# The last two token pairs before a block-product stage: two operand rests formed by TensorE and ScalarE

## The chip, the cores and the metric

The kernel runs on one core of one Trainium2 chip. The metric is the device time of one execution in microseconds, median over several runs. The engines are TensorE (PE, matmuls into PSUM), VectorE (DVE), ScalarE (ACT), GpSimd (POOL) and SyncE (SP, which issues most DMAs). Each engine works through its own instructions in a fixed order, and semaphores tie the engines together.

## The reference

Two layers of a sequence model over 1024 tokens of width 1024, in float32. Each layer has a token mixer (an S5 state-space mixer with a gated linear unit in layer 0, a gated short convolution in layer 1), a SwiGLU feed-forward block of hidden width 2816, and an embedding gated by the residual stream. Every part takes an RMS-normed copy of the residual stream `h` and adds its result to it:

```python
def swiglu_ffn(u, w_in, w_out):
    gate, up = jnp.split(u @ w_in, 2, axis=-1)
    return (jax.nn.silu(gate) * up) @ w_out
...
    for i in range(DEPTH):
        ...
        h = h + mix
        h = h + swiglu_ffn(rmsnorm(h, norm_ffn_g[i]), ffn_w_in[i], ffn_w_out[i])
        gate = jax.nn.sigmoid(rmsnorm(h, norm_ple_g[i]) @ ple_w_gate[i])
        h = h + gate * (p[i] @ ple_w_up[i])
```

## The kernel before

**Products in three terms.** A float32 operand x is kept as a pair: `hi`, x rounded to the type `fp32r` that PE multiplies, and the rest `lo = x - hi`. A product is then three matmuls (`mm3`, lines 124 to 126): hi by hi, hi by lo, lo by hi. `split` (line 89) makes such a pair: ACT casts x to `hi` (line 90), then DVE subtracts to give `lo` (line 91). Elsewhere, in the state-space part and for the embeddings, `split_pe` (line 289) makes it without DVE from an x that lies in PSUM: ACT casts (291), PE adds minus the identity times `hi` onto the same PSUM bank (292), ACT copies what is left to SBUF (293).

**Block products.** Three stages multiply by a large weight through a Strassen-like scheme of seven block products in place of eight: the input product of both feed-forward blocks (`ffn_in`) and that of the short convolution (`conv_in`). The moving side is the normed, transposed residual stream. The 1024 tokens are eight tiles of 128; tile q and tile q + 4 form pair q, and the 1024 channels are split in two halves. So each pair has four blocks p[row, half], each 128x512 in one PSUM bank, and from these come seven operands: p00; T2; T1; p01; T3; p11; T4, with b12 a copy of p10, T1 = b12 - p00, T2 = p11 - T1, T3 = p11 - b12, T4 = p01 - T2. Counted from 0, operand 3 is p01 (the fourth) and operand 5 is p11 (the sixth). `put(c, q, src)` (line 227) splits operand c of pair q into its place: operands 0 to 3 in `ulow`, 4 to 6 in `uhigh`. One product of `block_product` (line 349) reads one operand of all four pairs at once (512 columns), 12 matmuls for four slices of channels. Seven products accumulate in three PSUM banks a, b, c; the fourth product accumulates onto bank a after ACT has copied the first product out of it (lines 364 and 375).

The stationary side comes from `weights_set` (line 315): two raw tiles give seven weight operands in the same way, with four DVE additions (lines 335, 336, 338, 343) and seven splits (lines 90 and 91, tile name `ws`).

**Handing over from the stage before.** The stage ahead of each block-product stage finishes `h` tile by tile. `posted` (line 1314) then norms each tile and, once both tiles of a pair are there, `norm_pair` (line 220) makes that pair's operands beside the matmuls of the other tiles. Pairs 0 and 1 go this way. Pairs 2 and 3 (a and z) are left for `last_pairs` (line 256), which runs when the stage's last matmuls are over. It transposes (`transposed`, line 182, on PE with an identity, into PSUM), puts operand 0 of each pair, and steps two generators `others` (line 230) in turn: one step per operand from 1 to 6. It runs three times: ahead of the first feed-forward block, of the convolution and of the second feed-forward block.

PSUM tiles come from the pools `tr` (three banks) and `mm` (five banks, line 1290); the products' a, b, c come from `mm` too, and p01 of pair a and p00 and p01 of pair z lie there. The tiles b12, T1, T2, T3 and T4 share one SBUF pool `t2` with five buffers (line 1306).

**What sets the order.** The order of the instructions on each engine is not that of the code. A planner in the launch (line 1423, `schedule_with_timeline_sim=True`) works it out by a simulated timeline: earlier code has priority, `first()` and `tc.high_priority` raise it, and an instruction is placed once what it needs is there on that timeline. `tc.issue_after(ins)` forces the instructions in its block behind `ins` on that engine. `last_pairs` notes its last ACT instruction (`done["others"]`, line 271), and `weights_set` places the first weight operand of the stage's second set behind it (line 331). The first set's raw tiles are loaded ahead of the stage and its first operands have a raised priority.

Of the kernel before, what the change touches and what calls it, by code (L numbers as in the profile page):

```python
# [14 lines left out]
ALU = mybir.AluOpType  # L15
# [3 lines left out]
P = 128  # L19
# [5 lines left out]
def trunk(  # L25
# [8 lines left out]
    V, A, G, PE = nc.vector, nc.scalar, nc.gpsimd, nc.tensor  # L34
# [21 lines left out]
    ident = const.tile([P, P], F32, name="ident")  # L56
# [10 lines left out]
    KH = KT // 2  # L67
# [17 lines left out]
    def psum(pool=None):  # L85
        pool = pool or mm
        return pool.tile([P, 512], F32, name="ps" + pool.name, tag="ps")

    def split(hi, lo, src):
        A.copy(hi, src)  # L90
        V.tensor_tensor(lo, src, hi.bitcast(F32), ALU.subtract)  # L91
# [62 lines left out]
    def t2_tile(name, dt=F32, n=512):  # L154
        return t2.tile([P, n], dt, name=name, tag="t2")
# [14 lines left out]
    def normed(t, gb, halves=1, xn=None):  # L170
        with first():
            rs = norm_stat(t)
            if xn is None and early:
                turn.append(turn.pop(0))
                xn = raw_tile(turn[-1], name="xn")
            xn = raw_tile(name="xn") if xn is None else xn
            for c in range(halves):
                cs = slice(c * D // halves, (c + 1) * D // halves)
                V.scalar_tensor_tensor(xn[:, cs], h[t][:, cs], rs, gb[:, cs], ALU.mult, ALU.mult)
        return xn  # L180

    def transposed(xn, hf, pool=None):

        pt = psum(pool or tr)
        for c in range(KH):
            kt = hf * KH + c
            PE.transpose(pt[:, c * P:(c + 1) * P], xn[:, kt * P:(kt + 1) * P], ident)
        return pt

    def by_kt(a):  # L190
        return a.rearrange("p (c j) -> p c j", c=KH)
# [17 lines left out]
    def moving_part(c, l, q):  # L209

        if c < 4:
            return ulow[:, q].rearrange("p (c k l j) -> p c k l j", c=4, k=KH, l=2)[:, c, :, l, :]
        return uhigh[:, c - 4, :, l, q * P:(q + 1) * P]
# [6 lines left out]
    def norm_pair(q, gb):  # L220
        x0, x1 = normed(q, gb), normed(q + HT, gb)
        p = {(0, 0): transposed(x0, 0), (1, 0): transposed(x1, 0), (1, 1): transposed(x1, 1), (0, 1): transposed(x0, 1, mm)}
        put(0, q, p[0, 0])
        for _ in others(q, p):
            pass

    def put(c, q, src):
        split(moving_part(c, 0, q), moving_part(c, 1, q), by_kt(src))

    def others(q, p):  # L230

        b12 = t2_tile("b12")
        A.copy(b12, p[1, 0])
        T1 = t2_tile("T1")
        V.tensor_tensor(T1, b12, p[0, 0], ALU.subtract)
        T2 = t2_tile("T2")
        V.tensor_tensor(T2, p[1, 1], T1, ALU.subtract)
        put(1, q, T2)
        yield
        put(2, q, T1)  # L240
        yield
        put(3, q, p[0, 1])
        yield
        T3 = t2_tile("T3")
        V.tensor_tensor(T3, p[1, 1], b12, ALU.subtract)
        put(4, q, T3)
        yield
        put(5, q, p[1, 1])
        yield
        T4 = t2_tile("T4")  # L250
        V.tensor_tensor(T4, p[0, 1], T2, ALU.subtract)
        put(6, q, T4)

    done = {}

    def last_pairs(xs, gb):


        a, z = HT - 2, HT - 1
        with tc.issue_after(done["sum"]), tc.issue_after(done["square"]):  # L260
            p = {(0, 0): transposed(xs[a], 0), (1, 0): transposed(xs[a + HT], 0), (1, 1): transposed(xs[a + HT], 1),
                 (0, 1): transposed(xs[a], 1, mm)}
            put(0, a, p[0, 0])
            xs[z], xs[T - 1] = normed(z, gb, 2), normed(T - 1, gb, 2)
            r = {(0, i): transposed(xs[z], i, mm) for i in range(2)}
            put(0, z, r[0, 0])
            r.update({(1, i): transposed(xs[T - 1], i) for i in range(2)})
            pa, pz = others(a, p), others(z, r)
            for g in (pa, pa, pz, pz, pa, pz, pa, pz, pa, pz, pa, pz):
                next(g, None)  # L270
            done["others"] = next(i for i in reversed(tc.nc.cur_bb.bb.instructions) if i.engine == A.engine)
# [12 lines left out]
    def transposes(pt, parts):  # L284
        for c, a in enumerate(parts):
            PE.matmul(pt[:, c * P:(c + 1) * P], a, ident, start=c == 0, stop=True, is_transpose=True,
                      skip_group_check=c > 0)

    def split_pe(hi, lo, pt, view=lambda a: a):

        A.copy(hi, view(pt))
        PE.matmul(pt, identn, hi, start=False, stop=True, skip_group_check=True)
        A.copy(lo, view(pt))
# [568 lines left out]
    def small(shape=(P, NG), dt=F32):  # L862
        return st.tile(list(shape), dt, name="sm", tag="sm", bufs=28)
# [8 lines left out]
    def tt(o, a, b, op):  # L872
        V.tensor_tensor(o, a, b, op)
        return o
# [68 lines left out]
    for hf in range(2):  # L943
        pt = psum(tr)
# [5 lines left out]
    for hf in range(2):  # L950
        pt = psum(tr)
# [22 lines left out]
    r = small()  # L974
# [7 lines left out]
    z = tt(small(), r, r, ALU.mult)  # L982
# [331 lines left out]
    def posted(gain, pairs):  # L1314

        gb = load_gain(gain)
        xs = {}

        def post(t):
            if not pairs:  # L1320
                return norm_tile(t, gb)
            spill(t)
            if 0 < t < HT - 1:
                norm_pair(t - 1, gb)
            elif t == HT - 1:
                xs.update({i: normed(i, gb) for i in (HT - 2, T - 2)})
            elif t == T - 1:
                last_pairs(xs, gb)
        return post
# [98 lines left out]
```

## Time and profile before

| | us |
|---|---|
| median of 3 runs | 2269.39 |
| lowest and highest run | 2267.07, 2272.16 |
| the profiled execution | 2269.76 |
| its span, first to last instruction | 2267.8 |
| busy in the span: PE, DVE, ACT, POOL | 2168.0, 1644.6, 908.5, 358.7 |

Times in the profile's rows count from the start of the span. A row of the timeline gives the start, the duration, the engine, the line, the operation, output <- input, and in brackets the engine's idle time just before, with what ended it. A row of a group gives the count, the busy time with the mean duration of one, and the idle time before them. Buffer numbers are left out of names: `psmm` and `pstr` are tiles of the PSUM pools `mm` and `tr`, `T` stands for T1 to T4, `ws` for weight operands, `st` for sums of weights, `raw` for loaded weights. PE matmuls overlap, so their spacing, not their duration, is what one costs on a busy PE; the same holds to a smaller extent for DVE and ACT.

### The profile page before, as it was taken

The numbers are of one execution on the slowest core, as the hardware profiler recorded it, in microseconds if no ns is written. First come the engines' busy times: TensorE is split into PE (matmuls) and PEld (weight loads), VectorE is DVE, ScalarE is ACT, GpSimd is POOL, SyncE is SP. The second block draws the span as 40 slices with busy tenths as digits, with TensorE's granted clock in tenths as the row PEclk, the third lists the DMA queues.
The fourth block names the chain that finished last, engine by engine and source line by source line (L and its number), as shares of the span: only waits on it lengthen the run. The fifth ranks groups of instructions, "written<-read, shape, count | busy, mean of one in ns | idle before, by whom it ended". The sixth has DMA issues, their size and how long they took to land. (4 is left out here: it accounts for less than half of the span.)

```text
span 2267.8 us, 27890 instructions
## 1 busy us (share of the span) xinstructions
PE 2168.0 (96%) x10001; PEld 1785.5 (79%) x10001; DVE 1644.6 (73%) x2746; ACT 908.5 (40%) x1731; POOL 358.7 (16%) x440
## 2 busy tenths in 40 slices
PE   6997999899999999999979999989999999999998
PEld 5776888788888877878858888868888888787887
DVE  7785324877777787887588776497877777778864
ACT  6554322444444443335343332263444444333442
POOL 2111001011111112342010000110111111224210
PEclk8999999999999999999989999999999999999999
DMA  7655301344444477664232333723444445866713
GB/s 242 159 121 136 110 19 47 110 163 146 164 143 158 148 247 295 242 243 160 98 107 84 93 93 123 263 97 121 154 152 150 157 146 190 327 255 224 256 60 112
DMA packets 234010, 358.14 MB, mean 158 GB/s; under 512 B 23696, under 2 KB 166032, under 8 KB 233872
## 3 DMA queue, kind: packets, MB, share of 16 engines
q1 hardware_dynamic: 203040, 247.24, 33.6%
q0 software_dynamic: 30432, 109.08, 13.6%
q8 instruction: 79, 1.29, 0.2%
q14 instruction: 59, 0.48, 0.1%
q10 hardware_dynamic: 400, 0.04, 0.0%
HBM read 225.53 MB, written 114.29 MB: 150 GB/s over the span
## 5 line engine op out<-in xcount | busy, mean ns | idle before, releaser
L124 PE MATMUL psmm<-ulow,ws 128*128 128x512 f32 x896 | 352.3, 394 | 19.0 <-ACT ws L90 17.6
L126 PE MATMUL psmm<-ulow,ws 128*128 128x512 f32 x896 | 351.0, 392 | 3.1 <-DVE ws L91 3.1
L125 PE MATMUL psmm<-ulow,ws 128*128 128x512 f32 x896 | 351.7, 393 | 0.0
L124 PE MATMUL psmm<-uhigh,ws 128*128 128x512 f32 x672 | 261.4, 389 | 0.0
L125 PE MATMUL psmm<-uhigh,ws 128*128 128x512 f32 x672 | 261.4, 389 | 0.0
L126 PE MATMUL psmm<-uhigh,ws 128*128 128x512 f32 x672 | 261.4, 389 | 0.0
L90 ACT CAST ws<-raw 128x512 fp32r<-128x512 f32 x224 | 138.7, 622 | 265.8 <-PE psmm L126 245.6
L487 POOL DMA_DIRECT2D hw<-hs x154 | 115.9, 753 | 767.8 <-DVE hs L91 741.6
L124 PEld LDWEIGHTS psmm<-ulow,ws 128*128 128x128 f32 x896 | 170.3, 190 | 56.5 <-ACT ws L90 18.8
L126 PEld LDWEIGHTS psmm<-ulow,ws 128*128 128x128 f32 x896 | 169.8, 189 | 40.8 <-DVE ws L91 5.4
L125 PEld LDWEIGHTS psmm<-ulow,ws 128*128 128x128 f32 x896 | 170.2, 190 | 35.1
L629 DVE TENSOR_TENSOR h<-psmm,h 128x512 f32<-128x512 f32 x234 | 155.2, 682 | 45.6 <-PE psmm L126 25.6
L638 POOL TENSOR_TENSOR h<-part,h 128x512 f32<-128x512 f32 x100 | 139.1, 1394 | 242.6 <-ACT part L637 213.1
L124 PE MATMUL psmm<-ulow,w 128*128 128x512 f32 x380 | 150.8, 397 | 14.6 <-DVE h L629 10.0
L91 DVE TENSOR_TENSOR ws<-raw,ws 128x512 fp32r<-128x512 f32 x224 | 153.4, 687 | 4.7 <-ACT ws L90 4.6
L126 PE MATMUL psmm<-ulow,w 128*128 128x512 f32 x380 | 148.1, 390 | 0.0
L125 PE MATMUL psmm<-ulow,w 128*128 128x512 f32 x380 | 148.0, 389 | 0.0
L124 PEld LDWEIGHTS psmm<-uhigh,ws 128*128 128x128 f32 x672 | 126.2, 188 | 26.2
L125 PEld LDWEIGHTS psmm<-uhigh,ws 128*128 128x128 f32 x672 | 126.2, 188 | 26.1
L126 PEld LDWEIGHTS psmm<-uhigh,ws 128*128 128x128 f32 x672 | 126.2, 188 | 26.1
L90 ACT CAST ws<-st 128x512 fp32r<-128x512 f32 x168 | 103.8, 618 | 102.2 <-PE psmm L126 94.9
L124 PE MATMUL psmm<-w,ulow 128*128 128x512 f32 (+1 forms) x360 | 139.0, 386 | 0.0
(266 smaller groups left out, 4435.9 us busy)
## 6 DMA issues: line engine op xcount, KB each, us to landing
hw<-hs POOLq DMA_DIRECT2D x154, 512.0 KB, 4.2
w<-hw SPq DMA_DIRECT2D x88, 768.0 KB, 5.6
raw<-in_ffn_w_in_dram SPq DMA_DIRECT2D x88, 512.0 KB, 3.9
raw<-in_ffn_w_out_dram SPq DMA_DIRECT2D x44, 512.0 KB, 6.3
hd<-h POOLq DMA_DIRECT2D x24, 512.0 KB, 3.0
h<-hd SPq DMA_DIRECT2D x24, 512.0 KB, 5.9
raw<-in_conv_w_in_dram SPq DMA_DIRECT2D x24, 512.0 KB, 4.0
w<-hw SPq DMA_DIRECT2D x88, 128.0 KB, 5.5
```

The costliest lines, as they stand in the source:

```text
L90: A.copy(hi, src)
L91: V.tensor_tensor(lo, src, hi.bitcast(F32), ALU.subtract)
L124: PE.matmul(ps, ahi, bhi, start=start, stop=False, skip_group_check=more)
L125: PE.matmul(ps, ahi, blo, start=False, stop=False, skip_group_check=more)
L126: PE.matmul(ps, alo, bhi, start=False, stop=stop, skip_group_check=more)
L487: nc.gpsimd.dma_start(out=hidden[j][:, :, c].rearrange("q p l j -> p q l j"), in_=hs.bitcast(F32))
L629: done["sum"] = V.tensor_tensor(h[t][:, cs], ps, h[t][:, cs], ALU.add).ins
L638: G.tensor_tensor(h[t][:, cs], part, h[t][:, cs], ALU.add)
```

## The change

In `last_pairs` alone, the fourth and the sixth operand (p01 and p11) are split with `split_pe` in place of `split`. Since that overwrites the PSUM bank of p01, T4, which reads p01, is computed before the fourth operand is put instead of before the seventh; its own split stays where it was. T3, which reads p11, was already computed ahead of the sixth operand. `norm_pair` keeps the old way (`late` is false there).

`transposed` now goes through `transposes` (line 284), for all its callers: the same four transposes, where only the first of a bank carries the start flag.

```diff
     def transposed(xn, hf, pool=None):
 
         pt = psum(pool or tr)
-        for c in range(KH):
-            kt = hf * KH + c
-            PE.transpose(pt[:, c * P:(c + 1) * P], xn[:, kt * P:(kt + 1) * P], ident)
+        transposes(pt, [xn[:, (hf * KH + c) * P:(hf * KH + c + 1) * P] for c in range(KH)])
         return pt
...
-    def others(q, p):
+    def put_pe(c, q, src):
+        split_pe(moving_part(c, 0, q), moving_part(c, 1, q), src, by_kt)
+
+    def others(q, p, late=False):
 
         b12 = t2_tile("b12")
         A.copy(b12, p[1, 0])
...
         yield
         put(2, q, T1)
         yield
-        put(3, q, p[0, 1])
+        if late:
+            T4 = t2_tile("T4")
+            V.tensor_tensor(T4, p[0, 1], T2, ALU.subtract)
+            put_pe(3, q, p[0, 1])
+        else:
+            put(3, q, p[0, 1])
         yield
         T3 = t2_tile("T3")
         V.tensor_tensor(T3, p[1, 1], b12, ALU.subtract)
         put(4, q, T3)
         yield
-        put(5, q, p[1, 1])
+        (put_pe if late else put)(5, q, p[1, 1])
         yield
-        T4 = t2_tile("T4")
-        V.tensor_tensor(T4, p[0, 1], T2, ALU.subtract)
+        if not late:
+            T4 = t2_tile("T4")
+            V.tensor_tensor(T4, p[0, 1], T2, ALU.subtract)
         put(6, q, T4)
...
-            pa, pz = others(a, p), others(z, r)
+            pa, pz = others(a, p, True), others(z, r, True)
```

The functions that the change calls, as they stand:

```python
    def transposes(pt, parts):
        for c, a in enumerate(parts):
            PE.matmul(pt[:, c * P:(c + 1) * P], a, ident, start=c == 0, stop=True, is_transpose=True,
                      skip_group_check=c > 0)

    def split_pe(hi, lo, pt, view=lambda a: a):

        A.copy(hi, view(pt))
        PE.matmul(pt, identn, hi, start=False, stop=True, skip_group_check=True)
        A.copy(lo, view(pt))
```

## The prediction

> **What bounds the kernel now.** I read the page first (busy shares, then the costliest groups), then the window view around the three places where `last_pairs` runs, then the timeline there, engine by engine.
>
> ```profile
> span 2267.8 us, 27890 instructions
> L124 PE MATMUL psmm<-ulow,ws 128*128 128x512 f32 x896 | 352.3, 394 | 19.0 <-ACT ws L90 17.6
> ```
>
> The second row is the first matmul of each term of a block product. Before these 896 matmuls PE stood idle 19.0 us, and 17.6 us of that ended with an ACT cast of weights (line 90). The window view shows where. Columns: busy us and count of PE, PEld, DVE, ACT, POOL, then the granted clock.
>
> ```profile
> 401.00:428.00 27.00, 20.51 (x87) 15.23 (x85) 25.50 (x50) 16.48 (x31) 1.61 (x3) 0.81 0.35 109
> 1157.00:1182.00 25.00, 9.31 (x42) 7.13 (x41) 23.51 (x41) 14.05 (x27) 2.85 (x6) 0.61 0.33 112
> 1501.00:1535.00 34.00, 23.55 (x95) 17.73 (x95) 32.07 (x56) 19.12 (x34) 1.65 (x3) 0.80 0.26 81
> 428.00:800.00 372.00, 372.00 (x1641) 308.15 (x1642) 290.47 (x467) 156.04 (x268) 48.98 (x65) 1.00 0.45 149
> 1182.00:1460.00 278.00, 277.27 (x1221) 229.32 (x1221) 188.04 (x276) 81.21 (x125) 17.37 (x33) 1.00 0.39 126
> 1535.00:1950.00 415.00, 413.27 (x1823) 341.99 (x1822) 321.89 (x517) 173.02 (x296) 57.96 (x77) 1.00 0.49 160
> ```
>
> The first three rows are the handovers into a block-product stage (call them H1, H2, H3): DVE is busy nearly throughout (25.50 of 27.00, 23.51 of 25.00, 32.07 of 34.00 us), PE is not, and the clock is low. The last three rows are the stages behind them: PE is full (372.00 of 372.00), so what PE gains or loses in a handover stays to the end. Outside the handovers DVE time is worth nothing here. ACT has room (16.48 of 27.00 in H1).
>
> **The change, part by part.** Line 187's transposes become line 286's: the same instruction, number and size, only the start flag differs. I cost them at 0; they stay where they are on PE, so nothing covers them or needs to.
>
> Per handover, four DVE subtractions go (two pairs, fourth and sixth operand). They are 2 of the 3 in the first of these rows (H1, grouped by line and shape) and both in the second; the last two are from H2's timeline:
>
> ```profile
> L91 DVE TENSOR_TENSOR ulow<-psmm,ulow 128x512 fp32r<-128x512 f32 x3 | 2.0, 683 | 0.0
> L91 DVE TENSOR_TENSOR uhigh<-pstr,uhigh 128x512 fp32r<-128x512 f32 x2 | 1.4, 682 | 0.0
> ```
>
> ```profile
> 1178.65 0.68 DVE L91 TENSOR_TENSOR uhigh<-pstr,uhigh 128x512 fp32r<-128x512 f32 x1
> 1179.25 1.28 DVE L91 TENSOR_TENSOR uhigh<-T,uhigh 128x512 fp32r<-128x512 f32 x2
> ```
>
> The mean is 683 ns, but neighbours overlap: on the timeline they start 0.60 us apart (1178.65, 1179.25). So 4 x 0.60 = 2.4 us of DVE time go in each handover. Added are four PE matmuls and four ACT copies. The kernel does the same at lines 291 to 293 elsewhere (first two rows); the others are neighbouring matmuls of H3's timeline:
>
> ```profile
> L292 PE MATMUL pstr<-ulow,identn x24: 390/498/796, 8.6 to 222.5; 128*128 128x512 f32 x24
> L293 ACT CAST ulow<-pstr x24: 568/586/638, 9.4 to 225.8; 128x512 fp32r<-128x512 f32 x24
> ```
>
> ```profile
> 1523.51 0.39 PE L125 MATMUL psmm<-ulow,ws 128*128 128x512 f32 x1
> 1523.73 0.39 PE L126 MATMUL psmm<-ulow,ws 128*128 128x512 f32 x1
> ...
> 1530.80 0.63 PE L125 MATMUL psmm<-ulow,ws 128*128 128x512 f32 x1
> 1531.22 0.63 PE L124 MATMUL psmm<-ulow,ws 128*128 128x512 f32 x1
> ```
>
> A copy is 0.59 us on ACT. A matmul on a full PE costs its spacing: 0.22 us (1523.51 to 1523.73), 0.42 us at the low clock (1530.80 to 1531.22). T4 (line 251) isn't added; it moves ahead of the fourth operand, because the matmul overwrites the p it reads. No DMA moves.
>
> *H2: the plain case.*
>
> ```profile
> 1169.05 0.68 DVE L335 TENSOR_TENSOR st<-raw 128x512 f32<-128x512 f32 x1
> 1180.45 0.68 DVE L91 TENSOR_TENSOR ws<-raw,ws 128x512 fp32r<-128x512 f32 x1
> 1177.57 1.22 ACT L90 CAST uhigh<-T 128x512 fp32r<-128x512 f32 x2 [0.69 <-DVE T L251]
> 1178.69 0.61 ACT L90 CAST ws<-raw 128x512 fp32r<-128x512 f32 x1
> 1179.36 0.79 PE L124 MATMUL psmm<-ulow,ws 128*128 128x512 f32 x1 [11.19 <-ACT ws L90]
> ```
>
> PE waits 11.19 us for the first weight cast, which ACT starts the moment it is through with the seventh operand (1177.57), and that waits for T4 on DVE. Raw weights were there by 1169.05 (line 335 read them). DVE runs without a gap in front, so all four removed subtractions shorten the chain: 2.4 us. The added ACT and PE work lies in idle time (PE waits anyway). Bounds: 0, if a buffer and not this order holds the cast; 2.4. I take 2.4, since the cast follows its predecessor with no gap.
>
> *H1.* Two PE waits matter:
>
> ```profile
> 418.23 0.49 PE L124 MATMUL psmm<-ulow,ws 128*128 128x512 f32 x1 [0.68 <-ACT s L364]
> 427.94 0.50 PE L126 MATMUL psmm<-ulow,ws 128*128 128x512 f32 x1 [0.79 <-DVE ws L91]
> 416.39 0.68 DVE L91 TENSOR_TENSOR ulow<-T,ulow 128x512 fp32r<-128x512 f32 x1
> 427.21 0.68 DVE L91 TENSOR_TENSOR ws<-raw,ws 128x512 fp32r<-128x512 f32 x1
> ```
>
> The first says which product runs second: only the one on the fourth operand (line 375) accumulates onto the bank that line 364 copies. So the order is first, fourth, then the others, and the fourth operand has become urgent. Its rest now ends a longer chain. T4 needs one of the five `t2` buffers; if they are handed out in the order of the code (an inference), it is the one the second pair's T1 frees when its rest is done, 416.39 + 0.68 = 417.07 in H1. The two removed subtractions in front make that 1.2 us earlier, 415.9; then two T4 on DVE (1.2), the matmul (0.42), the copy (0.59) and the handoffs: about 418.2, as now. So nothing won or lost there. The 0.79 us wait for the second set's first rest (427.21) goes, because 2.4 us leave DVE ahead of it. Two matmuls then lie on a full PE: +0.45. H1: -0.3; bounds -1.2 (the whole earlier start counts) to +0.9 (four matmuls, the wait stays late).
>
> *H3.* Here the wait is larger:
>
> ```profile
> 1517.55 0.68 DVE L91 TENSOR_TENSOR ulow<-T,ulow 128x512 fp32r<-128x512 f32 x1
> 1525.37 1.27 DVE L251 TENSOR_TENSOR T<-psmm,T 128x512 f32<-128x512 f32 x2
> 1527.23 1.28 ACT L477 ACT_TABLE_LOAD   x1
> 1529.02 0.61 ACT L90 CAST uhigh<-T 128x512 fp32r<-128x512 f32 x1
> 1529.53 0.62 ACT L90 CAST ws<-raw 128x512 fp32r<-128x512 f32 x1
> 1515.62 0.50 PE L124 MATMUL psmm<-ulow,ws 128*128 128x512 f32 x1 [0.68 <-ACT s L364]
> 1530.20 0.80 PE L124 MATMUL psmm<-ulow,ws 128*128 128x512 f32 x1 [6.08 <-ACT ws L90]
> 1524.00:1530.00 6.00, 0.12 (x1) 0.00 (x0) 6.00 (x11) 4.59 (x8) 0.00 (x0) 0.80 0.16 47
> 1530.00:1534.50 4.50, 4.30 (x10) 3.44 (x11) 4.45 (x8) 0.67 (x2) 0.00 (x0) 0.51 0.03 6
> ```
>
> PE stops 6.08 us until the second set's first cast, which line 331 ties behind the last ACT instruction of the pairs: the cast of the last T4 (1529.02). That T4 runs at 1525.97 (second of the two from 1525.37), and then ACT fits in a table load. Afterwards PE runs ten matmuls at the low clock (0.51): 10 x (0.42 - 0.22) = 2.0 us more. In the changed order T4 runs when the second pair's T1 is done (1517.55, less 1.2, ends 1517.0), so both are over by 1518.3, 8 us earlier, and ACT has idle time for their casts ahead of the table load. Then 6.08 + 2.0 = 8.1 us of PE loss can go. Against it: the fourth operand's rest comes at about 1519.4, so the product on the third operand goes second; its operand is done at 1517.0, the start moves from 1515.62 to 1517.05, +1.4; four matmuls, +0.9. That leaves 5.8. PE will meet some next wait; I take one like H1's 0.79. H3: -5.0; bounds -7 and +2.3 (the wait stays, PE's additions are not hidden).
>
> By that shift PE idles 2.1 us at 1515 (from 1514.94, 0.68 ahead of 1515.62, to 1517.05). The Trainium skill ("TensorE: Matmul & The Clock Gate", Part 1) says that idling through a window of about 3.4 us halves the clock; the rows from 1524 agree. By its rule 2.1 us usually keep the clock and the sum stands; a drop would add the same 2.0 us.
>
> **Sum:** -2.4 - 0.3 - 5.0 = -7.7 us on the profiled execution's 2269.76 us (span 2267.8 and 2.0 around it): 2262.0. The runs' median, 2269.39, is 0.4 below that execution; I leave the forecast at 2262.0.
>
> **Rivals.**
> (a) *H3's wait stays.* If ACT still casts the last T4 after the table load, H3 gives about 0 and H1 and H2 stay: 2269.8 - 2.7 = 2267. For it: ACT's order is a planner's, and 1527.23 shows it puts other work first. Against: that cast waited for DVE until 1526.6.
> (b) *H2's cast is held by a buffer.* The weights' buffers lie where the last stage's tiles were. Then -5.3: 2264.5. Against: no gap before 1178.69.
> (c) *Slower: a matmul that waits at the head of PE's queue.* PE keeps its order, as the 6.08 us show: the work behind stood too. The sixth operand's matmul needs ACT's cast of p:
>
> ```profile
> 421.24 0.58 ACT L90 CAST uhigh<-pstr 128x512 fp32r<-128x512 f32 x1
> 1523.60 0.58 ACT L90 CAST uhigh<-pstr 128x512 fp32r<-128x512 f32 x1
> ```
>
> Queued behind the first product, it stops PE in H1 from 418.2 to 421.8: +3.6, +2.0 for a fallen clock, +0.45, -0.8 for the wait it swallows, so +5.2. In H3 it stops PE from 1517.05 to 1524.2; 40 matmuls at 0.22 and the clock's 2.0 end at 1535.0, against 1530.20 + 2.0 = 1532.2 now: +2.8. With H2's -2.4: +5.6, 2275.4. It decides where the planner takes that cast for done 3 us or more too early. Against: the cast itself waits for nothing but ACT, and can come early.
> (d) *It changes nothing net:* the planner fills DVE's freed time with weights needed later, 2269.
>
> **Chances.** Forecast 0.52, (a) 0.20, (b) 0.10, (c) 0.11, (d) 0.07. 0.2% is 4.5 us, about what a measurement of this kernel can tell from no change: faster means below 2264.9. Faster: 0.50 of the forecast's 0.52, two thirds of (b): 0.57. Slower: 0.11. Same: 0.32. The forecast alone spans 2259 to 2265. The range adds (a), (b) and (d) and, at the lower end, the 2.3 us by which the lowest run shown (2267.07) lies under the median: 2257 to 2270. It leaves out (c) and the far ends of H1 and H3 together.
>
> **What would show it.** Right: 12 fewer subtractions from psum on line 91 and 12 matmuls with identn; line 251 ahead of line 245 in each handover; the 11.19 us wait near 8.8; 6.08 below 2; the 17.6 us in the page's row near 10. Wrong: a PE wait of over 2 us in front of line 292 (c); a wait at the fourth operand after line 364 over 3 us with the clock at half; the last T4's cast still behind the table load (a).

## The result, and the profile after

| | before | after |
|---|---|---|
| median of 6 runs, us | 2269.39 | 2262.58 |
| lowest and highest | 2267.07, 2272.16 | 2260.70, 2264.11 |
| the profiled execution, its span | 2269.76, 2267.8 | 2263.69, 2261.9 |

The ratio is 0.9968, with a 95% interval of 0.9958 to 0.9979: 4.8 to 9.5 us faster. A second set of runs of the changed kernel (below) gave 2262.09 and 0.9955 to 0.9982. One run of that set took 3905.69 us and one of h12_only 9895.25, far above all others, and their medians here leave them out. The forecast was 2262.0. So the sum came out; the question is whether its terms did.

The page of the changed kernel, the rows that answer to the one shown of before:

```profile
span 2261.9 us, 27919 instructions
...
L124 PE MATMUL psmm<-ulow,ws 128*128 128x512 f32 x896 | 352.3, 394 | 3.7 <-ACT ws L90 3.7
L125 PE MATMUL psmm<-ulow,ws 128*128 128x512 f32 x896 | 351.5, 392 | 1.1 <-ACT ulow L300 1.1
```

The lines of the changed kernel are numbered otherwise than those of before: `transposes` is line 293 there, `split_pe` casts on ACT in line 298, subtracts on PE in line 299 and copies the rest on ACT in line 300; T4 is line 245 and T3 line 251.

The wait ahead of the 896 matmuls fell from 19.0 to 3.7 us; the prediction had its ACT part, 17.6, come near 10. Read alone, that promises 15 us. Under 7 came. Part of the wait has only changed its row, as PE's groups in H2's window show (changed kernel, 1157 to 1190 us):

```profile
L124 PE MATMUL psmm<-ulow,ws 128*128 128x512 f32 x13 | 6.0, 458 | 0.2 <-ACT ws L90 0.2
...
L299 PE MATMUL pstr<-uhigh,identn 128*128 128x512 f32 x2 | 1.6, 794 | 1.9 <-ACT uhigh L298 1.9
L299 PE MATMUL psmm<-ulow,identn 128*128 128x512 f32 x2 | 1.6, 792 | 6.3 <-ACT ulow L298 6.3
```

8.2 us of idle time now stand ahead of the new matmuls (6.3 and 1.9), where 11.19 stood ahead of the first product.

The change was made as read: in the groups of DVE's line 91, the subtractions from PSUM are 12 fewer, and T4 runs ahead of T3 in each handover. First before, then after:

```profile
L91 DVE TENSOR_TENSOR ulow<-psmm,ulow 128x512 fp32r<-128x512 f32 x15 | 10.1, 682 | 0.3 <-ACT ulow L90 0.3
L91 DVE TENSOR_TENSOR uhigh<-pstr,uhigh 128x512 fp32r<-128x512 f32 x12 | 8.2, 680 | 0.0
```

```profile
L91 DVE TENSOR_TENSOR ulow<-psmm,ulow 128x512 fp32r<-128x512 f32 x9 | 6.2, 684 | 0.3 <-ACT ulow L90 0.3
L91 DVE TENSOR_TENSOR uhigh<-pstr,uhigh 128x512 fp32r<-128x512 f32 x6 | 4.1, 685 | 0.0
```

**A yardstick by stages.** Runs of one kernel spread over 4 us and more, so each handover was measured on its own, from its first transposes to a point where PE has long been full: ACT's copy of the first product (line 364 of before, 371 after) of the ninth weight set in H1 and H3, of the seventh in H2. For H3, which is counted from the eight transposes that end PE's wait for `xn`, these are the ends, before and after:

```profile
1504.89 1.32 PE L187 MATMUL psmm<-ident,xn 128*128 128x128 f32 x8 [1.71 <-DVE xn L179]
...
1673.90 0.59 ACT L364 COPY s<-psmm 128x512 f32<-128x512 f32 x1 [0.91 <-PE psmm L126]
```

```profile
1505.17 1.32 PE L293 MATMUL psmm<-ident,xn 128*128 128x128 f32 x8 [1.71 <-DVE xn L179]
...
1669.19 0.59 ACT L371 COPY s<-psmm 128x512 f32<-128x512 f32 x1 [0.91 <-PE psmm L126]
```

So 169.01 us became 164.02. All profiles of this study, in us ("ahead" is the time up to H1's first transposes):

| kernel | ahead | H1 | H2 | H3 |
|---|---|---|---|---|
| before, two profiles | 401.5, 400.6 | 167.7, 169.3 | 138.0, 139.2 | 169.0, 169.6 |
| changed, two profiles | 398.8, 399.0 | 169.0, 168.4 | 138.0, 139.3 | 164.0, 164.0 |
| h3_only | 400.1 | 168.3 | 138.2 | 164.9 |
| t4_early | 399.5 | 167.3 | 138.6 | 165.0 |
| fourth_only | 400.6 | 168.1 | 137.6 | 165.5 |
| sixth_only | 400.3 | 167.1 | 138.2 | 167.1 |
| no_tie | 398.9 | 167.1 | 138.4 | 165.2 |
| h12_only | 399.2 | 167.9 | 138.8 | 166.7 |
| ws_low | 398.8 | 167.7 | 136.2 | 165.9 |
| ws_low_b | 399.9 | 168.5 | 136.0 | 167.4 |
| ws_low_notie | 400.7 | 167.9 | 136.3 | 164.8 |

Between the means of the two pairs of profiles the span fell by 6.8 us: 5.3 in H3, nothing in H1 and H2 (0.2 and 0.1 longer), 2.2 ahead of H1, and the rest lost 0.4. Ahead of H1 every engine's order of instructions is the same in all these kernels; 398.8 to 401.5 is the spread of 13 profiles there. The 2.2 us lie within that spread, so these runs do not show them to be the work of the change.

### The profile page after: what moved, and what is told of

The parts are those of the page before. It is cut to its first block, busy times and chain, and to the rows that moved or that the text cites. A ratio compares the mean times of both kernels' runs of the same rounds, so it can differ in the third digit from the quotient of the medians.

```text
span 2261.9 us, 27919 instructions
## 1 busy us (share of the span) xinstructions
PE 2170.9 (96%) x10013; PEld 1785.7 (79%) x10013; DVE 1639.3 (72%) x2734; ACT 915.1 (40%) x1743; POOL 358.9 (16%) x440
## 4 chain that ended last, share of the span: by engine, by line
PE 82%; DVE 6%; DMA 3%; ACT 1%; issue 1%; SPq 0%; DVEq 0%; POOLq 0%; ACTq 0%; POOL 0%
PE psmm L124 27%; PE psmm L126 26%; PE psmm L125 26%; DMA hw<-hs 1%; DVE ulow L91 1%; DVE h L636 1%; DMA w<-hw 1%; PE pstr L202 1%; PE pstr L293 1%; DVE uhigh L91 0%; DVE xn L179 0%; DVE hs L91 0%; PE pstr L1245 0%; PE pstr L1247 0%; PE pstr L1246 0%
## 5 line engine op out<-in xcount | busy, mean ns | idle before, releaser
L90 ACT CAST ws<-raw 128x512 fp32r<-128x512 f32 x224 | 139.2, 624 | 264.8 <-PE psmm L126 254.2
L645 POOL TENSOR_TENSOR h<-part,h 128x512 f32<-128x512 f32 x100 | 139.2, 1395 | 243.9 <-ACT part L644 215.8
```

The source lines that it names most:

```text
L645: G.tensor_tensor(h[t][:, cs], part, h[t][:, cs], ALU.add)
```

## The experiments

Each ran in five rounds beside the kernel before. Ratios are to before, with their 95% interval. The edits of no_tie and sixth_only are shown against before, the others against the changed kernel.

**before_again and after_again** are the two kernels unaltered.

> The kernel before once more, for a second profile of it: the first 400 us have the same order of instructions in every kernel here, yet took 398.8 to 401.5 us in the profiles so far. If that is chance from execution to execution, this profile's stretch ahead of the first handover lies anywhere from 398.5 to 401.5, the third handover and eight weight sets behind it again take 169.0 within 0.5, and the waits of 11.19 and 6.08 us stand. If the profile of before was itself out of the ordinary in the third handover, the 6.08 us wait is another.

> The changed kernel once more: more runs and a second profile. By the stages of its first profile the first handover cost 0.9 us more than before, the second nothing, the third gained 5.0. If so, the first handover's stretch is 168.9 within 0.5 again (before 167.7 and 168.3), the second's 138.0, the third's 164.0, and the median 2263 to 2265; if its median of 2262.6 stands, the run's difference of 6.8 us is larger than the handovers explain.

Measured: 2270.11 (ratio 0.9993 to 1.001) and 2262.09 (0.9955 to 0.9982), below the 2263 to 2265 that the handovers alone would give. H3 repeats within 0.6 us, the waits of 11.19 and 6.08 came again as 11.19 and 5.87; the same order of instructions gives H1 and H2 stretches that differ by 1.6 and 1.3 us. A difference of under 1.5 us in one stretch of one profile therefore says little.

**h3_only**: the change in the third handover alone.

```diff
+    handover = []
...
+        handover.append(len(handover) + 1)
...
-            pa, pz = others(a, p, True), others(z, r, True)
+            late = handover[-1] in (3,)
+            pa, pz = others(a, p, late), others(z, r, late)
```

> The change in the third handover alone (late is true only in the third call of last_pairs); the first two keep the old pairs. Theory A (the whole gain is the 6.08 us wait of the third handover and the low clock behind it, released because T4 and its cast come early): 5 to 6.5 us faster than before, about 2263.5, as fast as the whole change or up to 1 us faster; in the third handover no PE wait over 2 us, the first two as before (11.19 us wait in the second). Rival B (every handover gains about 2 us from the DVE subtractions that go): only about 2 us, 2267.5.

Measured: 2264.50, 0.9970 to 0.9987: 4.6 us faster, a little under the 5 to 6.5 expected. Up to H3 every engine's order is that of before, and H3 takes 164.9: most of the gain is there without the other two handovers.

**h12_only**: the same edit with `(1, 2)`.

> The change in the first and second handover alone (late is true in the first two calls of last_pairs), the third as before. Theory A (in the second handover four ACT copies and two trips through PE take the place of four DVE subtractions in front of the first weight cast, and the first handover breaks even): no gain, 2268 to 2270.5; the first product of the second handover starts 22.1 us after its first transpose, as in the changed kernel (before: 21.7), the third keeps a wait of 5.5 to 6.5 us. The forecast's step (2.4 us less in the second, 0.3 in the first): 2266.5, first product after some 19.5 us.

Measured: 2265.03, 0.9973 to 0.9991: 3.7 us faster, and neither theory had that. The second handover is as theory A had it: the first product starts 22.1 us after the first transpose (1154.72, 1176.82). The gain lies in H3, which took 166.7, though its code is that of before. PE's wait there, from the timeline:

```profile
1525.61 0.47 PE L124 MATMUL psmm<-uhigh,ws 128*128 128x512 f32 x1 [3.65 <-ACT uhigh L90]
1526.16 0.80 PE L124 MATMUL psmm<-ulow,ws 128*128 128x512 f32 x1
```

PE now does products of the first set on `uhigh` while the second set is late; before, it stood 6.08 us in front of that set. The planner works on a simulated time line, and an edit 350 us upstream was enough for another order here. The kernel ws_low_b, whose third handover is likewise untouched, has such an order too (167.4). So about 2 us of H3 can be had or lost by the planner's order alone.

**t4_early**: T4 ahead of the fourth operand, both splits with DVE as before.

```diff
-            put_pe(3, q, p[0, 1])
-        else:
-            put(3, q, p[0, 1])
+        put(3, q, p[0, 1])
...
-        (put_pe if late else put)(5, q, p[1, 1])
+        put(5, q, p[1, 1])
```

> T4 is computed ahead of the fourth operand in all three handovers, as in the change, but both operands keep the split with DVE: no subtraction goes, no matmul and no ACT copy is added. Theory A: the tied cast of the third handover still comes some 5 to 7 us earlier, the 6.08 us wait shrinks below 2 us, and 4 to 6 us are gained: 2263.5 to 2265.5. Rival B (DVE's lighter load is what pays): no gain, 2268.5 to 2270.5, the 6.08 us wait stays above 4 us.

Measured: 2264.59, 0.9977 to 0.9994; H3 165.0. Four of the 5.3 us come with no subtraction removed. The 6.08 us wait is gone; what is left is this one:

```profile
1523.82 0.50 PE L125 MATMUL psmm<-ulow,ws 128*128 128x512 f32 x1 [1.65 <-DVE ulow L91]
```

It is the fourth operand's rest, which DVE makes here. In the changed kernel, where it comes from ACT, the wait at this place is 1.14 us.

**no_tie**: before, without the tie of the second set's first cast.

```diff
-        with tc.issue_after(second) if second else tc.high_priority(offset=400) if ahead else ExitStack():
+        with tc.high_priority(offset=400) if ahead else ExitStack():
             w11 = operand(a11)
```

> The kernel before without the tie that sets the first weight cast of the second set behind the last ACT instruction of the pairs; nothing else differs. Theory A: that tie is what PE waited for in the third handover, so its 6.08 us wait and the low clock behind it go at least in part: 2262 to 2266, the second handover as before. Rival C (the second set's products wait for something else behind T4, the PSUM bank that holds p01 or DVE's weight sums, and the cast only came last): the wait stays above 4 us, 2268 to 2271.

Measured: 2263.26, 0.9968 to 0.9987; H3 165.2. The tie was what held PE, and without it the kernel is about as fast as the changed one. Behind it stands a smaller wait, and here the late T4 itself holds PE, as the timeline of this kernel shows:

```profile
1522.72 1.28 DVE L251 TENSOR_TENSOR T<-psmm,T 128x512 f32<-128x512 f32 x2
1523.46 0.50 PE L124 MATMUL psmm<-ulow,ws 128*128 128x512 f32 x1 [2.37 <-DVE T L251]
```

T4 reads p01 in PSUM (`psmm`), and the product that waits takes a bank of the same pool, which is the likely reason: of the wait that rival C put down to T4's side, 2.37 us are there. In the changed kernel neither wait is left.

**sixth_only**: the sixth operand alone on TensorE and ScalarE, T4 late.

```diff
-        put(5, q, p[1, 1])
+        (put_pe if late else put)(5, q, p[1, 1])
```

> Only the sixth operand is split with TensorE and ScalarE; T4 and the fourth operand stay as before. Half of the subtractions go (2 in each handover). Theory A: the last T4 comes at most 1.2 us earlier in the third handover, so the wait there stays at 4.5 us or more, and the total is 2268 to 2270.5. Rival B: about half of the whole change's gain, 2265.5 to 2267.

Measured: 2264.13, 0.9970 to 0.9990: a miss of 4 us. H3 is 167.1, not 169: the order of the planner changed as in h12_only, and PE's waits there are 0.59, 1.21 and 0.59 us with some 13 matmuls at the low clock behind them. The stretches give 2.2 us for H3 and 1.4 for H1, and the latter is no more than two profiles of one kernel differ by; how the rest of the 4.9 us is spread was not settled. It does not speak for rival B: H2 is 138.2.

**fourth_only**: T4 early, the fourth operand on TensorE and ScalarE, the sixth with DVE.

```diff
-        (put_pe if late else put)(5, q, p[1, 1])
+        put(5, q, p[1, 1])
```

> T4 early and the fourth operand on TensorE and ScalarE as in the change, the sixth operand with DVE as before. Theory A: the tied cast is early, so the third handover gains as in the changed kernel, 4 to 5.3 us (its stretch 164.0 to 165.0); in the second handover two ACT copies fewer and two DVE subtractions more than in the changed kernel balance, first product 21.5 to 22.5 us after the first transpose; 2262.5 to 2265.5. Rival B (each removed subtraction pays): half of the changed kernel's gain, 2266.

Measured: 2263.28, 0.9968 to 0.9985; H3 165.5, first product of H2 21.6 us after the first transpose (1157.43, 1179.04). The time and this start are as theory A had them; H3 is 0.5 above its range.

**ws_low and ws_low_b**: the order of the pools in the convolution's input stage, in the changed kernel and in before.

```diff
-    inner("c", conv_in, (("cv", 2), ("hs", 2), ("ea", 1), ("st", 3), ("pad", 1), ("ws", (1, 8, 0)), ("eb", 1)))
+    inner("c", conv_in, (("ws", (1, 8, 0)), ("st", 3), ("cv", 2), ("hs", 2), ("ea", 1), ("pad", 1), ("eb", 1)))
```

> The changed kernel with the pools of the convolution's input stage stacked in another order: the weight operands come to lie over the last stage's weights and no longer over the spilled h tiles. Theory A (in the second handover PE waits only for where the first weight cast stands in ACT's order, behind the four added copies): the cast comes ahead of the pairs' casts, the first product starts some 10 us earlier, operands gate it then as in the other handovers, and 4 to 8 us are gained on the changed kernel: 2255 to 2260. Rival B (the operands themselves are late, the cast only last in line): the first product starts earlier, the next ones wait, gain under 2 us.

> The kernel before with the same new order of pools. By theory A 4 to 8 us faster than before, 2261 to 2265, and between this and the changed kernel with the new pools lies the same 5 to 6 us of the third handover; the second handover is within 1.5 us of that one's, in either direction. If the change's shorter DVE chain (2.4 us) pays in the second handover once the weight cast is out of its way, this one's second handover is 1.5 to 2.5 us longer than the changed kernel's with the new pools.

Measured: 2256.91 (0.9934 to 0.9959), faster than both kernels, and 2263.48 (0.9962 to 0.9985). H2 in the timeline of ws_low:

```profile
1155.32 0.60 PE L293 MATMUL pstr<-ident,xn 128*128 128x128 f32 x4
1156.56 1.12 ACT L90 CAST ws<-raw 128x512 fp32r<-128x512 f32 x2
1165.36 0.80 PE L124 MATMUL psmm<-ulow,ws 128*128 128x512 f32 x1
1172.81 0.73 PE L124 MATMUL psmm<-ulow,ws 128*128 128x512 f32 x2 [2.65 <-ACT ws L90]
```

The weight casts now come beside the stage's last matmuls and the first product starts 10.0 us after the first transpose instead of 22.1. Twelve us earlier at the start are worth only about 2.4 in the stretch, for other weights gate PE next (2.65 us here) and then an operand (1.70 at a matmul of line 299). So the total fell in theory A's range, while the handover behaved more as rival B had it. With the weights out of the way, H2 is the same with and without the change (136.2, 136.0), so its shorter DVE chain does not pay here either. ws_low's profile is its slowest run (2260.09), so its stretches explain less than the median's 5.2 us against the changed kernel; how the rest is spread was not settled.

**ws_low_notie**: ws_low and no_tie's edit together.

> The changed kernel with the new order of pools and without the tie of the second set's first cast. Theory A: in the third handover the tie no longer ends a wait once T4 is early, so taking it away adds nothing there; in the second handover the second set's raw tiles come late by DMA anyway: 2255.5 to 2258.5, within 1.5 us of the kernel with the new pools alone. Rival: the tie still costs in the second handover, 2253 to 2255.

Measured: 2259.46, 0.9942 to 0.9970, above what was expected, but its interval overlaps that of ws_low and its time ahead of H1 was 1.9 us longer; H2 is equal and H3 1.1 shorter. Once T4 is early the tie costs nothing that can be seen.

## Why the prediction was right, and where it was wrong

**H3: right, in mechanism and size** (forecast -5.0, measured -5.3). The chain, in the timeline of the changed kernel (the last four rows are for the second paragraph below):

```profile
1517.83 0.69 DVE L245 TENSOR_TENSOR T<-psmm,T 128x512 f32<-128x512 f32 x1
1519.63 0.69 DVE L245 TENSOR_TENSOR T<-psmm,T 128x512 f32<-128x512 f32 x1
1521.64 0.63 ACT L90 CAST uhigh<-T 128x512 fp32r<-128x512 f32 x1
1522.16 0.63 ACT L90 CAST ws<-raw 128x512 fp32r<-128x512 f32 x1
1526.87 1.28 ACT L484 ACT_TABLE_LOAD   x1
1516.81 0.72 PE L124 MATMUL psmm<-ulow,ws 128*128 128x512 f32 x2 [1.55 <-ACT ws L90]
1524.89 0.50 PE L125 MATMUL psmm<-ulow,ws 128*128 128x512 f32 x1 [1.14 <-ACT ulow L300]
1514.34 0.62 ACT L90 CAST ulow<-T 128x512 fp32r<-128x512 f32 x1 [0.58 <-DVE T L238]
1514.82 0.69 DVE L91 TENSOR_TENSOR ulow<-T,ulow 128x512 fp32r<-128x512 f32 x1
1516.14 0.62 ACT L90 CAST ws<-st 128x512 fp32r<-128x512 f32 x1 [0.26 <-DVE st L345]
1517.22 0.69 DVE L91 TENSOR_TENSOR ulow<-T,ulow 128x512 fp32r<-128x512 f32 x1
```

The last T4's cast (1521.64) and the tied cast behind it (1522.16) come ahead of the table load, 7.4 us earlier than before. The left-over wait is 1.14 (forecast 0.8), and the clock held through it. The second T4 ended at 1520.3, not by 1518.3, since the planner put work on weights between the two, and the second fourth operand's rest came from ACT at 1524.25, not 1519.4. Neither cost more than that 1.14.

Two steps behind these numbers were not as the prediction had them. PE goes on at 1516.81 (forecast 1517.05), but what it waited for was the cast at 1516.14 of a weight sum (line 345, the weights of the second operand), not the third operand's rest. One matmul on the second operand goes first, and the product on the third follows behind it. The third operand was ready sooner: the rest at 1517.22 is that of the second pair's T2, cast at 1514.34, and that pair's T1 rest is the one at 1514.82, or an earlier one. So the agreement of the start is luck. Nor is the inference on the `t2` buffers shown: on DVE the first T4 starts 1.2 us after the start of the second pair's T1 rest in H2, but at least 2.4 us after it in H1 and 3.0 in H3, with other work between. No run had another number of buffers.

h3_only, t4_early and no_tie show the cause of the 6.08 us wait: the tie behind a late T4. The size is less certain than the forecast's hit suggests. With T4 late and the tie in place H3 took 166.7 to 169.6 us in five profiles, with T4 early 164.0 to 165.9 in seven. All seven are shorter, but how much of the 5.3 us is T4's and how much the planner's order, which other edits change as well, these runs do not separate.

**H2: wrong** (forecast -2.4, measured +0.1, with 1.3 between two profiles of one kernel; the first product starts 0.4 us later, 22.1 in place of 21.7 us after the first transpose, in both profiles of each kernel). The step that failed is "The added ACT and PE work lies in idle time (PE waits anyway)". PE was idle, but ACT was in the chain: it runs in its order, and the first weight cast stands behind the copies. ACT's timeline in the changed kernel:

```profile
1176.16 0.59 ACT L300 CAST ulow<-psmm 128x512 fp32r<-128x512 f32 x1
1176.64 0.63 ACT L90 CAST uhigh<-T 128x512 fp32r<-128x512 f32 x1
1177.16 0.59 ACT L298 CAST uhigh<-pstr 128x512 fp32r<-128x512 f32 x1
1177.63 0.60 ACT L300 CAST ulow<-psmm 128x512 fp32r<-128x512 f32 x1
1178.11 0.65 ACT L90 CAST uhigh<-T 128x512 fp32r<-128x512 f32 x1
1178.63 0.61 ACT L298 CAST uhigh<-pstr 128x512 fp32r<-128x512 f32 x1
1179.11 0.62 ACT L300 CAST uhigh<-pstr 128x512 fp32r<-128x512 f32 x1
1179.58 0.66 ACT L90 CAST ws<-raw 128x512 fp32r<-128x512 f32 x1
```

ACT has no gap from 1176.16 to the cast; three of the four added copies lie in that row. Before, ACT waited for DVE at this place. DVE's chain became shorter and ACT's took over at the same length. The trade is even: with no copy added and no subtraction removed (t4_early) the first product starts 22.2 us after the first transpose, with half of each (fourth_only) 21.6, with all (the changed kernel) 22.1. The sign that the prediction named, 11.19 us near 8.8, would have passed for the idle time as a whole: PE's is 8.4 (8.2 and 0.2, above). But the four new matmuls, each some 0.8 us at the low clock, fill the difference, and the cast came no sooner. The start of the first product is the mark to read. Rival (b) gave this total for H2, with another mechanism: no buffer held the cast on the chip, since ACT runs into it without a gap. The buffers decided where the planner placed the cast, and ws_low shows what that was worth.

**H1: the size fits within the noise** (forecast -0.3 within -1.2 to +0.9, measured +0.2, where two profiles of one kernel differ by up to 1.6), **the path was not right.** The fourth operand was taken to stay second. As in H3, a matmul on the second operand and then the product on the third went ahead of it, after these waits for the cast of the same weight sum, in the changed kernel's first and second profile:

```profile
414.83 1.22 PE L124 MATMUL psmm<-ulow,ws 128*128 128x512 f32 x2 [1.19 <-ACT ws L90]
```

```profile
414.63 0.73 PE L124 MATMUL psmm<-ulow,ws 128*128 128x512 f32 x2 [2.91 <-ACT ws L90]
```

The DVE wait of 0.79 went as forecast; these waits, at ACT's weight cast, took its place and that of the 0.68 at the copy.

**The sum**: -7.7 forecast, -6.8 and -6.9 measured in the two sets of runs, but in the profiles only -5.0 lies in the three handovers. The 2.4 us that H2 did not give were made up, in these profiles, by 2.2 us ahead of H1, which the change does not touch. That the total came out nearer than its terms is luck.

**The rivals.** (a): no, the last T4's cast lies ahead of the table load. (c): PE waits ahead of line 299 only in H2, where it waited anyway; in H1 and H3 the new matmuls came with no wait. (d): no, H3 gained. That the planner's choice moves the time by some us all the same is what h12_only and sixth_only showed.

## What to carry to other kernels

When work moves from a full engine to one that "has room", follow the receiving engine's order up to the instruction the path waits for: its mean load says nothing if the moved work stands in front of it. Judge a handover by when the first product starts and by a mark well behind it, for idle time can move to another row. Where a planner orders the work, test a local edit with everything upstream unaltered, and repeat the profile, before a few us are credited to it.

## What the runs showed of the hardware

A short PE wait can cost more than its length. In the timeline of h3_only a wait of 1.71 us was over at 1515.11, and the clock fell after it:

```profile
1515.11 0.74 PE L124 MATMUL psmm<-ulow,ws 128*128 128x512 f32 x2 [1.71 <-ACT ws L90]
1515.68 0.39 PE L125 MATMUL psmm<-ulow,ws 128*128 128x512 f32 x1
1515.91 0.60 PE L126 MATMUL psmm<-ulow,ws 128*128 128x512 f32 x1
1516.31 0.63 PE L124 MATMUL psmm<-ulow,ws 128*128 128x512 f32 x1
...
1519.29 0.49 PE L125 MATMUL psmm<-ulow,ws 128*128 128x512 f32 x1
```

From 1515.91 to 1519.29, 3.4 us, the spacing is 0.43 in place of 0.23: eight matmuls, some 1.6 us lost. The wait of 1.55 us at the same place of the changed kernel (1516.81, above) cost no such stretch. The window view (busy us and count of PE, PEld, DVE, ACT, POOL, then the granted clock) shows how near the two cases are: first h3_only, in the 3.4 us ahead of the fall and the 3.4 behind it, then the changed kernel, in the two times 3.4 us that follow its own last low stretch.

```profile
1512.60:1516.00 3.40, 1.69 (x8) 0.94 (x7) 3.40 (x7) 1.62 (x3) 0.00 (x0) 0.99 0.00 0
1516.00:1519.40 3.40, 3.40 (x10) 2.62 (x10) 3.40 (x7) 1.77 (x4) 0.00 (x0) 0.51 0.53 154
```

```profile
1514.30:1517.70 3.40, 1.85 (x8) 1.21 (x8) 3.40 (x7) 1.82 (x3) 0.00 (x0) 1.00 0.00 0
1517.70:1521.10 3.40, 3.40 (x17) 2.77 (x16) 3.40 (x7) 2.55 (x5) 0.00 (x0) 1.00 0.52 154
```

PE was busy 1.69 us of the first 3.4 in h3_only, and the clock fell to 0.51; in the changed kernel it was busy 1.85, and the clock stayed. The Trainium skill ("TensorE: Matmul & The Clock Gate", Part 1) has the clock fall after an idle window of about 3.4 us and calls that window free-running. The 3.4 us of the low stretch agree; that a window in which PE was busy for half of the time is enough does not, and there the rows decide.

The moment alone can decide too, as a place ahead of H1 shows. The sixteen matmuls that form `pb` stand in one order in all kernels; they took 2.05 us in six of the 13 profiles and 2.7 to 3.6 in the other seven. Here the changed kernel, then h3_only, after the same wait of 2.17 us:

```profile
65.37 2.05 PE L1211 MATMUL pb<-U,wbt 128*128 128x128 f32 x16 [2.17 <-ACT wbt L1162]
```

```profile
64.95 3.38 PE L1214 MATMUL pb<-U,wbt 128*128 128x128 f32 x16 [2.17 <-ACT wbt L1165]
```
